# Gate and up products of the two-stream feed-forward blocks by seven half-size products per pair, in a two-layer hybrid diffusion backbone

## The chip, the cores and the metric

One Trainium2 core runs the whole network in one launch. The metric is the device time of that launch in microseconds (us), smaller being better. Engines are named as in the profile: PE is the matrix engine (TensorE), PEld its weight loads, DVE the vector engine, ACT the scalar engine, POOL is GpSimd, and SP issues the DMAs.

## The reference

Two token streams of 256 tokens each (contexts `cx`, latents `x`), 1024 channels and two layers with the same weights for both streams; everything is float32. Cut to what matters here:

```python
for layer in range(DEPTH):                       # 2
    mx = jnp.split((silu_c @ ada_w[layer] + ada_b[layer])[:, None, :], N_MOD, axis=-1)   # 9 modulations, latents
    mc = ...                                     # the same from silu_cc, contexts
    x  = x  + 0.5 * mx[2] * swiglu(modulate(rmsnorm(x,  norm_w[layer, 0]), mx[0], mx[1]), ffn1_wgu[layer], ffn1_wd[layer])
    cx = cx + 0.5 * mc[2] * swiglu(modulate(rmsnorm(cx, norm_w[layer, 0]), mc[0], mc[1]), ffn1_wgu[layer], ffn1_wd[layer])
    ...                                          # mixer: retention and gated DeltaNet, gates, output projection
    x  = x  + 0.5 * mx[8] * swiglu(...)          # second FFN; the contexts only where the layer is not the last
return rmsnorm(x, final_norm_w)

def swiglu(h, w_gu, w_down):                     # w_gu: 1024 x 5632, w_down: 2816 x 1024
    gate, up = jnp.split(h @ w_gu, 2, axis=-1)
    return (jax.nn.silu(gate) * up) @ w_down
```

Three of the four feed-forward blocks work on both streams: first and second of layer 0, first of layer 1. They are called FFN(0,0), FFN(0,2) and FFN(1,0) here. FFN(1,2) works on the latents alone.

## The kernel before, in words

Activations lie feature-major: a tile is 128 channels by 512 columns, the contexts in columns 0 to 255 and the latents in 256 to 511. A float32 product is made from three fast ones. Every operand is split into a rounded part hi and the rest lo, and hi times hi, hi times lo and lo times hi are added in PSUM; so each weight tile of 128 by 128 costs three matmuls (`dense`).

Weights come as a stream in the order of use. A DMA brings a unit of 1024 columns (tile `raw`, or two arena tiles `s`), that is two quanta of 512 columns, four weight tiles each. `_ensure` splits quanta ahead of PE: ACT copies the quantum to `wh` (rounded), and DVE subtracts it (`wl <- raw, wh`, L343). Splits run four quanta (`AHEAD`) ahead of the products. For one phase of the mixers every second `wl` is made on POOL (`plo`).

The hidden layer of 2816 has 22 column blocks in two halves of 11. For each half, 11 pairs of a gate block and its up block are made (two blocks of 8 channel tiles, 24 matmuls each, four quanta a pair), then `silu(gate) * up` is split, then the 8 down products of that half (22 quanta) are added to the residual `x` (`x_add`). During the last two down blocks of a feed-forward block (`tail`) and the first products of the next phase (`head`) the two streams run one after the other, so that the next norm is made meanwhile.

The modulations (one row of 1024 channels per layer, index and stream) are made beside the products: `ada_spread` is a generator that `run` interleaves with the products. For each of 8 channel tiles, two halves and two streams it issues one DVE instruction on 512 columns (`s <- s,sc,s`: accumulate a weight tile times a scalar per partition), and yields `GAP` us (1.5 to 2.0) of products. 32 such items, then a few small matmuls, make one modulation. 15 modulations are listed by phase in `SPREAD`.

Instructions reach each engine's queue in the order in which the Python code issues them, and an engine takes its queue in order.

The helpers hold the profile's lines: L274 every matmul, L262 every ACT instruction, L265 and L268 DVE's two-input and scalar-two-input instructions, L343 the `wl` of weights, L723 the sums of squares on POOL.

## Time and profile before

| | us |
|---|---|
| median of 3 runs (2434.14 to 2443.7) | 2438.14 |
| span of the profiled execution | 2433.8 |
| median less that span | 4.3 |

The page gives each engine's busy time over the whole span: PE 98%, PEld 84%, DVE 63%, ACT 41%, POOL 10%. A busy share is an average over phases that differ: feed-forward blocks with 512 columns to a matmul, mixers with many small products, and a last feed-forward block with 256 columns. The windows and the timeline separate them. A matmul's own duration in the profile overlaps with the next one's, so its rate is read from how many there are in a stretch, or from the distance of two instructions that wait for it.

### The profile page before, as it was taken

What the parts mean: (1) busy time and instruction counts of PE and PEld (TensorE: products, weight loads), DVE (VectorE), ACT (ScalarE), POOL (GpSimd) and SP (SyncE); (2) the same over time, 40 slices, a digit from 0 to 9 for tenths busy, and PEclk for the clock granted to TensorE, in tenths of its full rate; (3) what the DMA queues carried; (4) which work ended last, traced back from release to release, by engine and by line L of the source; (5) the groups of instructions that cost most, each with busy time, mean ns of one, the idle gap of its engine ahead of it and who ended that gap; (6) DMA issues with size and microseconds to landing.
All of it is one profiled execution on the core that took longest, in us unless ns stands there. A gap on an engine that the chain in (4) does not pass through costs nothing.

```text
span 2433.8 us, 38580 instructions
## 1 busy us (share of the span) xinstructions
PE 2389.8 (98%) x14930; PEld 2037.7 (84%) x14930; DVE 1529.1 (63%) x2905; ACT 1002.2 (41%) x1998; POOL 241.5 (10%) x256
## 2 busy tenths in 40 slices
PE   7999999999999999999999999999999899999998
PEld 5888888888778888888887897888897789999998
DVE  5776777536775655576656666556465648777654
ACT  4322224344645444342223342223254446555544
POOL 0000001012430200100000100000013322200001
PEclk9999999999999999999999999999999999999999
DMA  8545444322332414444444344444233424546653
GB/s 288 182 172 180 170 156 136 96 87 83 99 97 64 120 44 172 140 141 145 147 159 145 125 144 153 158 139 139 95 112 111 118 96 139 153 138 226 196 177 122
DMA packets 173848, 338.56 MB, mean 139 GB/s; under 512 B 49312, under 2 KB 54240, under 8 KB 173664
## 3 DMA queue, kind: packets, MB, share of 16 engines
q1 hardware_dynamic: 171264, 331.86, 41.2%
q10 hardware_dynamic: 2400, 4.23, 0.6%
q8 instruction: 117, 1.92, 0.3%
q14 instruction: 67, 0.55, 0.1%
HBM read 325.77 MB, written 10.26 MB: 138 GB/s over the span
## 4 chain that ended last, share of the span: by engine, by line
PE 91%; DVE 4%; issue 2%; DMA 2%; ACT 1%; POOL 0%; SPq 0%; DVEq 0%; ACTq 0%; POOLq 0%
PE mm L274 80%; PE mx L274 10%; DVE s L265 1%; DVE s L268 1%; PE mx L278 1%; ACT s L262 1%; DMA raw<-in_w_dram 1%; DVE wl L343 1%; DMA s<-gd 0%; POOL s L1349 0%; ACT wh L262 0%; DVE s L1368 0%; DMA s<-in_x_dram 0%; DVE sub L265 0%; DVE s L723 0%
## 5 line engine op out<-in xcount | busy, mean ns | idle before, releaser
L274 PE MATMUL mm<-s,wh 128*128 128x512 f32 (+1 forms) x6674 | 1785.3, 356 | 3.3 <-ACT s L262 1.6
L274 PEld LDWEIGHTS mm<-s,wh 128*128 128x128 f32 x6674 | 1169.1, 189 | 195.2 <-issue 9.1
L274 PE MATMUL mm<-s,wl 128*128 128x512 f32 (+1 forms) x3337 | 1180.7, 354 | 1.4 <-DVE wl L343 1.3
L274 PEld LDWEIGHTS mm<-s,wl 128*128 128x128 f32 x3337 | 629.5, 189 | 95.5 <-DVE wl L343 2.1
L262 ACT ACTIVATE s<-s 128x512 fp32r<-128x512 f32 (+4 forms) x555 | 274.9, 503 | 612.1 <-DVE s L265 405.4
L343 DVE TENSOR_TENSOR wl<-raw,wh 128x512 fp32r<-128x512 f32 x563 | 399.8, 719 | 101.6 <-ACT wh L262 66.6
L262 ACT ACTIVATE wh<-raw 128x512 fp32r<-128x512 f32 x622 | 374.3, 625 | 207.1 <-PE mm L274 144.0
L268 DVE SCALAR_TENSOR_TENSOR s<-s,sc,s 128x512 f32<-128x512 f32 x420 | 303.4, 748 | 0.0
L262 ACT ACTIVATE s<-mm 128x512 f32<-128x512 f32 (+2 forms) x177 | 91.3, 516 | 353.0 <-PE mm L274 352.3
L265 DVE TENSOR_TENSOR s<-s,s 128x512 fp32r<-128x512 f32 (+3 forms) x300 | 169.1, 575 | 44.7 <-ACT s L262 41.1
L274 PE MATMUL mx<-s,s 32*32 32x32 f32 (+3 forms) x2680 | 183.2, 243 | 11.0 <-DVE s L265 6.2
L274 PEld LDWEIGHTS mx<-s,s 32*32 32x32 f32 (+2 forms) x2680 | 168.9, 142 | 26.6 <-issue 13.4
L265 DVE TENSOR_TENSOR s<-s,mm 128x512 f32<-128x512 f32 (+1 forms) x88 | 54.6, 621 | 210.7 <-PE mm L274 207.5
L343 DVE TENSOR_TENSOR wl<-s,wh 128x512 fp32r<-128x512 f32 x233 | 164.3, 710 | 25.5 <-ACT wh L262 15.3
L723 POOL TENSOR_TENSOR s<-s,s 128x512 f32<-128x512 f32 (+1 forms) x31 | 38.0, 1226 | 1379.1 <-ACT s L262 1037.8
L262 ACT ACTIVATE wh<-s 128x512 fp32r<-128x512 f32 x234 | 140.4, 622 | 75.1 <-PE mm L274 67.8
L268 DVE SCALAR_TENSOR_TENSOR s<-mm,mods,s 128x256 f32<-128x256 f32 x132 | 58.9, 479 | 123.5 <-PE mm L274 123.4
L343 POOL TENSOR_TENSOR wl<-raw,wh 128x512 fp32r<-128x512 f32 x59 | 78.5, 1333 | 219.9 <-ACT wh L262 196.7
L268 DVE SCALAR_TENSOR_TENSOR s<-mm,par,s 128x508 f32<-128x508 f32 (+3 forms) x128 | 90.7, 711 | 13.7 <-ACT s L262 11.1
L262 ACT ACTIVATE s<-mx 128x256 f32<-128x256 f32 (+5 forms) x122 | 53.5, 447 | 76.2 <-PE mx L274 59.4
L274 PE MATMUL mm<-wh,s 128*128 128x512 f32 x256 | 81.2, 398 | 1.3 <-DVE s L977 1.1
L274 PE MATMUL mm<-s,s 128*128 128x256 f32 (+1 forms) x624 | 82.1, 291 | 0.0
(158 smaller groups left out, 1108.5 us busy)
## 6 DMA issues: line engine op xcount, KB each, us to landing
raw<-in_w_dram SPq DMA_DIRECT2D x318, 512.0 KB, 3.6
s<-in_ada_dram SPq DMA_DIRECT2D x288, 256.0 KB, 4.9
s<-in_w_dram SPq DMA_DIRECT2D x244, 256.0 KB, 5.3
s<-in_tab_dram SPq DMA_DIRECT2D x18, 256.0 KB, 4.0
xd<-s SPq DMA_DIRECT2D x16, 256.0 KB, 3.8
s<-gd ACTq DMA_DIRECT2D x16, 256.0 KB, 5.0
s<-in_x_dram SPq DMA_DIRECT2D x8, 256.0 KB, 5.4
yd<-s SPq DMA_DIRECT2D x8, 256.0 KB, 3.7
```

The costliest lines, as they stand in the source:

```text
L262: return self.nc.scalar.activation(out, in_, f, **kw)
L265: return self.nc.vector.tensor_tensor(out, a, b, op)
L268: return self.nc.vector.scalar_tensor_tensor(out, a, s, b, op0=op0, op1=op1)
L274: return self.nc.tensor.matmul(out, lhsT, rhs, start=start, stop=stop, **kw)
L278: return self.nc.tensor.transpose(out, in_, self.ident[:n, :n])
L343: eng.tensor_tensor(lo, self.raw[s // 2][0][s % 2], hi.bitcast(F32), ALU.subtract)
L723: eng.tensor_tensor(acc[:, n0:n1], acc[:, n0:n1], s[:, n0:n1], ALU.add)
```

## The change

Lines of the changed kernel are those of its own file: matmuls are L341, ACT L329, DVE's L332 and L335, the weights' `wl` L457.

For 49 of the 66 pairs of the three two-stream blocks, gate and up of a column block are made as a 2 by 2 block product (rows: gate, up; inner: even and odd channel tiles; columns: contexts, latents) by seven half-size products instead of eight, Strassen's scheme in Winograd's form. `FAST` gives the number of pairs that stay as they were: 11 and 0 in the halves of FFN(0,0), 3 and 0 in FFN(0,2) and in FFN(1,0). Each of the seven (`pairs`) has four channel tiles, three matmuls each, and 256 columns. Its weights are one of a11, a12, a22 (as they come) or one of four sums s1 to s4 that POOL makes from the raw weights (`_sum`, issued `LEAD` quanta ahead of the split). So a pair has seven quanta to split instead of four. Its activations are the tiles of one stream, or sums over streams and even and odd tiles that `xforms` makes once for each feed-forward block: 16 POOL instructions of 256 columns and 8 splits. Two PSUM tiles per pair, `a` and `b`, collect the products; `a` is copied out by ACT in between, while it goes on collecting.

The modulations become one list for the whole kernel. `background` advances it by time after each step of the products of a feed-forward block, at `gap` 1.6 or 1.8 us per item in plain pairs, 6.0 in the new pairs and 1.1 in the down products; in the down products every second item goes to ACT and POOL (`bgpool`). Up to 7 modulations are made in FFN(0,0) and in the first part of the first mixer (gap 3.0), the others in FFN(0,2) and FFN(1,0).

```diff
-SPREAD = {(0, 0): [(0, 2), (0, 3), (0, 4), (0, 5), (0, 6), (0, 7)], (0, 2): [(0, 8), (1, 0), (1, 1), (1, 2), (1, 3)],
-          (1, 0): [(1, 4), (1, 5), (1, 6), (1, 7)], (1, 2): []}
-GAP = {(0, 0): 1.5, (0, 2): 1.8, (1, 0): 2.0, (1, 2): 2.0}
+FAST = {(0, 0): (11, 0), (0, 2): (3, 0), (1, 0): (3, 0)}
+FORMS = ("a11", "a12", "s2", "s1", "s3", "s4", "a22")
+LEAD = 3
+SPREAD = [(0, i) for i in range(2, 9)] + [(1, i) for i in range(8)]
+RATE = (1.8, 6.0, 1.1), True
+RATES = {(0, 0, 0): ((1.6, 6.0, 1.1), True)}
+MIX_RATE = 3.0
+FIRST_MODS = 7
...
+    def _sum(self, s):
...
+        while self.presum and self.presum[0][0] <= s + LEAD:
+            _, u, f = self.presum.popleft()
+            d = self.sums[u]
+            (a11, a12), (a21, a22) = self.raw[u][0], self.raw[u + 1][0]
+            a, b, op = {"s1": (a21, a22, ALU.add), "s2": (d.get("s1"), a11, ALU.subtract),
+                        "s3": (a11, a21, ALU.subtract), "s4": (a12, d.get("s2"), ALU.subtract)}[f]
+            d[f] = self.A()
+            self.nc.gpsimd.tensor_tensor(d[f], a, b, op)
...
-            self.act(hi, src)
+            self._sum(s)
+            self.act(hi, self._src(s))
...
-            eng.tensor_tensor(lo, self.raw[s // 2][0][s % 2], hi.bitcast(F32), ALU.subtract)
+            eng.tensor_tensor(lo, self._src(s), hi.bitcast(F32), ALU.subtract)
...
+                        if st and self.bgpool:
+                            t = self.A() if k else a
+                            self.act(t, raw, AF.Copy, scale=c)
+                            if k:
+                                self.nc.gpsimd.tensor_tensor(a, a, t, ALU.add)
+                                self.Fr(t)
+                        elif k:
+                            self.stt(a, raw, c, a)
...
+    def xforms(self):
...
+        sub = lambda o, a, b: self.nc.gpsimd.tensor_tensor(o, a, b, ALU.subtract)
+        for i in range(5):
...
+                sub(p[:, lc], e[:, rc], e[:, lc])
+                sub(p[:, rc], o[:, rc], p[:, lc])
+                sub(r[:, lc], o[:, rc], e[:, rc])
+                sub(r[:, rc], o[:, lc], p[:, rc])
+                self.Fr(e, o)
+            if pend:
+                self.X.append([self.split(t, 0, 512, 0, 1) for t in pend])
...
+    def pairs(self, n, hid):
...
+            a, b = self.mm()[:, lc], self.mm()
+            g, c = self.A(), self.A()
...
+            prod(a, even, lc, True, False)
+            self.act(g[:, lc], a)
+            yield 1.42
+            prod(b[:, lc], odd, lc, True, False)
+            yield 1.42
+            prod(a, x1, rc, False, False)
+            self.act(g[:, rc], a)
+            yield 1.42
+            prod(b[:, rc], x1, lc, False, False)
+            self.act(c[:, rc], b[:, rc])
+            yield 1.42
+            prod(a, x2, lc, False, False)
+            self.act(c[:, lc], a)
+            self.nc.gpsimd.tensor_tensor(c[:, lc], c[:, lc], c[:, rc], ALU.add)
+            yield 1.42
+            prod(b[:, rc], odd, rc, False, True)
+            self.tt(g, g, b, ALU.add)
+            post.append(lambda: self.act(g, g, AF.Silu))
+            yield 1.42
+            prod(a, x2, rc, False, True)
+            self.nc.gpsimd.tensor_tensor(g[:, rc], g[:, rc], c[:, lc], ALU.mult)
+            self.tt(g[:, lc], g[:, lc], a, ALU.mult)
+            self.Fr(c)
+            hid.append(self.split(g, 0, 512, 0.5, 1))
+            yield 1.42
...
-            yield from self.dense([1] * 22 if half else G_FFN if l + j else G_START, KD, self.hk, n0, n1, ev)
+            rate, pool = RATES.get((l, j, half), RATE)
+            fast = (l, j) in FAST
+            self.gap, self.bgpool = rate[0], False
+            if fast and half == 0:
+                self.xgen = self.xforms()
+            for w in self.dense(_plain_groups(l, j, half), KD, self.hk, n0, n1, ev):
+                if fast and self.xgen:
+                    self.xgen = next(self.xgen, 0) is None and self.xgen
+                yield w
...
+                self.gap = rate[1]
+                yield from self.pairs(HH - _plain(l, j, half), hid)
+            self.gap, self.bgpool = rate[2], pool
```

What PE has in its queue in the second half of FFN(0,2), before (`s` are the split activations, `mm` the PSUM tile of one block, `wh` and `wl` one quantum of weights):

```order
L274 MATMUL mm_12326<-s10_9746,wh_12210 128x512
L274 MATMUL mm_12326<-s70_9747,wh_12210 128x512
L274 MATMUL mm_12326<-s10_9746,wl_12239 128x512
L274 MATMUL mm_12326<-s30_9766,wh_12210 128x512
L274 MATMUL mm_12326<-s8_9767,wh_12210 128x512
L274 MATMUL mm_12326<-s30_9766,wl_12239 128x512
```

The same place after the change, from a pair's fourth product to its fifth, where `mm_13977` and `mm_13976` are the collecting tiles `b` and `a` of one pair:

```order
L341 MATMUL mm_13977<-s29_11103,wh_13933 128x256
L341 MATMUL mm_13977<-s51_11104,wh_13933 128x256
L341 MATMUL mm_13977<-s29_11103,wl_13957 128x256
L341 MATMUL mm_13976<-s22_10956,wh_13953 128x256
L341 MATMUL mm_13976<-s75_10957,wh_13953 128x256
L341 MATMUL mm_13976<-s22_10956,wl_13984 128x256
```

Each matmul has half the columns, and 84 of them stand where 48 stood; each quantum of `wh` and `wl` still serves 12 matmuls.

DVE's queue at the same place before, about one pair long (`sc` marks an item of a modulation, `s49_12228,mm_12236` is silu(gate) times up):

```order
L343 TENSOR_TENSOR wl_12239<-s23_12018,wh_12210 128x512
L268 SCALAR_TENSOR_TENSOR s21_12179<-s26_12175,sc_164,s21_12179 128x512
L343 TENSOR_TENSOR wl_12256<-s25_12019,wh_12237 128x512
L265 TENSOR_TENSOR s49_12228<-s49_12228,mm_12236 128x512
L268 SCALAR_TENSOR_TENSOR s71_12181<-s26_12175,sc_164,s71_12181 128x512
L343 TENSOR_TENSOR wl_12282<-s34_12059,wh_12254 128x512
L265 TENSOR_TENSOR s61_12276<-s49_12228,s48_12275 128x512
L268 SCALAR_TENSOR_TENSOR s1_12180<-s63_12176,sc_164,s1_12180 128x512
L268 SCALAR_TENSOR_TENSOR s54_12182<-s63_12176,sc_164,s54_12182 128x512
L343 TENSOR_TENSOR wl_12305<-s57_12060,wh_12280 128x512
```

And after, one pair of the second half of FFN(0,2) (`s45_13978,mm_13977` adds PSUM tile `b`, `s45_13978,mm_13976` multiplies by `a`, `s58_14119` is the lo of the hidden tile):

```order
L457 TENSOR_TENSOR wl_14062<-raw_13734,wh_14042 128x512
L457 TENSOR_TENSOR wl_14082<-s30_13981,wh_14060 128x512
L332 TENSOR_TENSOR s45_13978<-s45_13978,mm_13977 128x512
L457 TENSOR_TENSOR wl_14101<-s42_13954,wh_14080 128x512
L332 TENSOR_TENSOR s45_13978<-s45_13978,mm_13976 128x256
L457 TENSOR_TENSOR wl_14128<-s37_14001,wh_14097 128x512
L335 SCALAR_TENSOR_TENSOR s68_13619<-s53_13950,sc_164,s68_13619 128x512
L457 TENSOR_TENSOR wl_14151<-s15_14020,wh_14124 128x512
L332 TENSOR_TENSOR s58_14119<-s45_13978,s36_14118 128x512
L457 TENSOR_TENSOR wl_14170<-raw_13770,wh_14147 128x512
L457 TENSOR_TENSOR wl_14189<-raw_13879,wh_14166 128x512
L457 TENSOR_TENSOR wl_14206<-raw_13879,wh_14187 128x512
```

Seven `wl` stand between two hidden tiles instead of four, one or two modulation items instead of six or so, and a second instruction that reads PSUM.

POOL has nothing in its queue before in the pairs; after, in the second half of FFN(0,2) (L405 are the sums s1 to s4 of the next pair's weights, L1078 the sum of two halves of `c`, L1085 the product with silu(gate) for the latents):

```order
L1078 TENSOR_TENSOR s21_12952<-s21_12952 128x256
L405 TENSOR_TENSOR s7_13070<-s43_12865,s58_12866 128x512
L1085 TENSOR_TENSOR s15_12951<-s15_12951,s21_12952 128x256
L405 TENSOR_TENSOR s34_13097<-s7_13070,s67_12814 128x512
L405 TENSOR_TENSOR s53_13117<-s67_12814,s43_12865 128x512
L405 TENSOR_TENSOR s42_13136<-s9_12815,s34_13097 128x512
L1078 TENSOR_TENSOR s74_13095<-s74_13095 128x256
```

Each pair has come to have four POOL instructions of 512 columns and two of 256.

## Rows read from the trace of the kernel before

**Rows 1.** The page: span, and busy time (share) and instructions of each engine.

```profile
span 2433.8 us, 38580 instructions
PE 2389.8 (98%) x14930; PEld 2037.7 (84%) x14930; DVE 1529.1 (63%) x2905; ACT 1002.2 (41%) x1998; POOL 241.5 (10%) x256
```

**Rows 2.** The page: the chain that ended last, shares by engine.

```profile
PE 91%; DVE 4%; issue 2%; DMA 2%; ACT 1%; POOL 0%; SPq 0%; DVEq 0%; ACTq 0%; POOLq 0%
```

**Rows 3.** Windows: down FFN(0,2), pairs FFN(0,2), pairs FFN(1,0), FFN(1,2), first mixer's start.

```profile
core 0: us, PE busy (x) PEld busy (x) DVE busy (x) ACT busy (x) POOL busy (x), PEclk, DMA share, GB/s
1166.00:1221.00 55.00, 55.00 (x252) 44.15 (x252) 33.33 (x61) 12.58 (x20) 0.00 (x0) 1.00 0.50 170
1232.00:1346.00 114.00, 114.00 (x517) 91.07 (x516) 70.67 (x122) 33.17 (x60) 0.00 (x0) 1.00 0.45 156
1610.00:1724.00 114.00, 114.00 (x518) 91.14 (x517) 67.33 (x113) 33.06 (x60) 0.00 (x0) 1.00 0.39 130
2250.00:2390.00 140.00, 140.00 (x1190) 140.00 (x1189) 83.59 (x152) 69.56 (x139) 0.00 (x0) 1.00 0.57 185
410.00:620.00 210.00, 210.00 (x1091) 175.83 (x1089) 110.82 (x194) 95.37 (x199) 27.78 (x25) 1.00 0.26 83
```

**Rows 4.** Timeline of DVE, a pair of FFN(0,2): start, length, idle before and its releaser.

```profile
1277.78 0.69 DVE L265 TENSOR_TENSOR s<-s,mm 128x512 f32<-128x512 f32 x1 [3.46 <-PE mm L274]
1278.38 0.75 DVE L268 SCALAR_TENSOR_TENSOR s<-s,sc,s 128x512 f32<-128x512 f32 x1
1279.04 0.68 DVE L343 TENSOR_TENSOR wl<-raw,wh 128x512 fp32r<-128x512 f32 x1
1279.64 0.68 DVE L265 TENSOR_TENSOR s<-s,s 128x512 fp32r<-128x512 f32 x1
...
1288.91 0.69 DVE L265 TENSOR_TENSOR s<-s,mm 128x512 f32<-128x512 f32 x1 [3.46 <-PE mm L274]
```

**Rows 5.** Timeline of DVE, a pair of FFN(1,2) (latents alone, 256 columns).

```profile
2353.03 0.42 DVE L265 TENSOR_TENSOR s<-s,mm 128x256 f32<-128x256 f32 x1 [1.20 <-PE mm L274]
2353.37 0.68 DVE L343 TENSOR_TENSOR wl<-s,wh 128x512 fp32r<-128x512 f32 x1
...
2358.69 0.42 DVE L265 TENSOR_TENSOR s<-s,mm 128x256 f32<-128x256 f32 x1 [1.20 <-PE mm L274]
```

**Rows 6.** Timeline of POOL and DVE, end of the first mixer.

```profile
1008.31 4.70 POOL L723 TENSOR_TENSOR s<-s,s 128x512 f32<-128x512 f32 x3 [79.14 <-ACT s L262]
1009.05 1.10 DVE L343 TENSOR_TENSOR wl<-s,wh 128x512 fp32r<-128x512 f32 x1
1010.35 1.50 DVE L343 TENSOR_TENSOR wl<-s,wh 128x512 fp32r<-128x512 f32 x1 [0.20 <-ACT wh L262]
```

**Rows 7.** Timeline of POOL and DVE in the second mixer.

```profile
1836.00 1.30 POOL L343 TENSOR_TENSOR wl<-raw,wh 128x512 fp32r<-128x512 f32 x1 [1.32 <-ACT wh L262]
1835.15 2.42 DVE L268 SCALAR_TENSOR_TENSOR s<-mm,par,s 128x510 f32<-128x510 f32 x4
```

**Rows 8.** Groups by line and shape, whole span: count, busy us, mean ns, idle before.

```profile
L723 POOL TENSOR_TENSOR s<-s,s 128x256 f32<-128x256 f32 x12 | 9.5, 796 | 229.5 <-ACT s L262 229.3
L262 ACT ACTIVATE wh<-raw 128x512 fp32r<-128x512 f32 x622 | 374.3, 625 | 207.1 <-PE mm L274 144.0 <-DMA raw<-in_w_dram 47.4 <-DVE wl L343 7.5
L262 ACT ACTIVATE s<-mm 128x256 f32<-128x256 f32 x66 | 25.0, 379 | 39.0 <-PE mm L274 38.9
```

**Rows 9.** The page: DMA issues of the weights, KB each, us to landing.

```profile
raw<-in_w_dram SPq DMA_DIRECT2D x318, 512.0 KB, 3.6
```

More of the change, by code (lines that the diff above doesn't have):

```diff
@@ L227, in __init__ @@
         self.nunits = ins["w"].shape[0]
+        self.plan = _plan(self.nunits)
+        self.nplan = len(self.plan)
+        self.nfreed, self.npre = 0, 0
+        self.sums, self.presum = {}, deque()
+        self.keepv, self.vs, self.xgen = False, {}, None
+        self.ready = set()
+        self.gap, self.bgt = None, 0.0
+        self.bgpool, self.bgmax = False, FIRST_MODS
+        self.bg = self.ada_spread()
         self.raw, self.hl = {}, {}
@@ L478, in head, with background @@
         self.steps = None
+    def background(self, dt):
+        if self.gap is None or self.bg is None:
+            return
+        self.bgt -= dt
+        while self.bgt <= 0 and self.bg:
+            w = next(self.bg, None)
+            if w is None:
+                self.bg = None
+            else:
+                self.bgt += w
     def run(self, dense, *mixers, scale=1.0):
@@ new lines, in ada_spread, with load @@
+    def ada_spread(self):
+        nxt, todo = [], deque((n, l, i, half, k) for n, (l, i) in enumerate(SPREAD) for half in range(2) for k in range(8))
+        def load():
+            if todo and todo[0][0] < self.bgmax:
+                _, l, i, half, k = todo.popleft()
+                nxt.append(self.A())
+                self.nc.sync.dma_start(nxt[-1], self.ins["ada"][l, i, k, half])
+        for l, i in SPREAD:
+            while not nxt:
+                load()
+                load()
+                yield 2.0 if nxt else 0.7
+            s = self.A()
+            for half in range(2):
+                acc = self.As(2)
+                for k in range(8):
+                    raw = nxt.pop(0)
+                    for st in range(2):
+                        a, c = acc[st], self.sc[:, k, st:st + 1]
+                        if st and self.bgpool:
[6 more added lines that the diff above has]
+                            self.stt(a, raw, c, a)
+                        else:
+                            self.nc.vector.tensor_scalar_mul(a, raw, c)
+                        yield self.gap
+                    self.Fr(raw)
+                    load()
+                yield 1.0
+                ps = self.mx()
+                for st in range(2):
+                    for j in range(2):
+                        p = 64 * half + 32 * j
+                        self.mat(ps[p:p + 32, 0:256], self.sel[:, st], acc[st][:, j * 256:j * 256 + 256], st == 0, st == 1)
+                self.Fr(*acc)
+                self.nc.vector.tensor_copy(s[64 * half:64 * half + 64, :256], ps[64 * half:64 * half + 64, :256])
+            self.ada_rows(l, i, s)
+            yield self.gap
```

191 lines of the change are left out of this document (139 added, 52 removed).

## The prediction

> **What bounds the kernel now.** I read the page first. PE is busy 98% of a span of 2433.8 us [rows 1], and the chain that ended last runs through PE for 91% [rows 2]; DVE has 63% and POOL 10%, so over the whole span PE is the bound and nothing else is near. The windows say the same of the stretches that change: in the pairs of FFN(0,2) and FFN(1,0) PE is busy for all 114 us, DVE for 70.67 and 67.33 of them, ACT for 33, POOL for none [rows 3]. The timeline gives the rate. DVE's multiplication by the up block waits for PE, and one pair later does so again: from 1277.78 to 1288.91, 11.13 us for 48 matmuls of 512 columns [rows 4]. FFN(1,2) has the same pairs with 256 columns: from 2353.03 to 2358.69, 5.66 us for 48 matmuls [rows 5], and PE is busy for all 140 us of its window, with as many weight loads [rows 3]. So half the columns cost half the time (0.118 us a matmul against 0.232), and DVE and ACT keep up with a quantum every 1.41 us.
>
> **A pair by PE alone.** 84 matmuls at 0.118 us are 9.91 us instead of 11.13: 1.22 us a pair, 59.8 us for 49 pairs. Nothing can give more, since the small matmuls of the modulations only move. The Trainium skill (TensorE: Matmul & The Clock Gate, Part 3, The mechanism) says that a weight load overlaps running matmuls only where the row groups differ. Here all are 128 by 128, so by it loads and matmuls would add: by the same page (Part 2, LDWEIGHTS) 128 columns at 1.2 GHz, an estimated 0.107 us more for each of 84, and the sum would be 9 us a pair longer than mine. The window of FFN(1,2) does not agree: 1190 matmuls and 1189 loads within 140 us leave no time between them [rows 3]. I take the row.
>
> **A pair by DVE and POOL together.** This term decides. At the end of the first mixer three POOL additions stand in one row of 4.70 us, and the two `wl` of DVE beside them take 1.10 and 1.50 us [rows 6] instead of 0.68 [rows 4]. In the second mixer a POOL instruction of the same size takes 1.30 us beside DVE instructions that read PSUM, which take 2.42 us for four, as fast as alone [rows 7]. So a DVE instruction with both inputs in SBUF and a POOL instruction don't run at once. What each holds the other up for: 4.70 less 1.30 is 3.40 for two rounds of one `wl` and one addition, 1.70 a round. A `wl` behind another DVE instruction comes 0.60 us before the next (1279.04 to 1279.64), a modulation item 0.66 (1278.38 to 1279.04) [rows 4]. That leaves 1.10 for a POOL instruction of 512 columns. One of 256 takes 0.80 [rows 8], 0.50 less than 1.30, so 0.60.
>
> In a new pair DVE has seven `wl` and the lo of the hidden tile, 8 x 0.60 = 4.80; modulation items, 7 steps of 1.42 us at one per 6.0, 1.6 x 0.66 = 1.06; POOL has four sums, 4.40, and two halves, 1.20. Together 11.46 us, more than PE's 9.91 and more than the 11.13 of before. Besides, DVE reads PSUM twice, 0.60 [rows 4] and 0.34 [rows 5]; POOL may work meanwhile if it has something ready. So a pair that goes on and on costs 11.46 to 12.40. I take 11.6, near the lower end, since POOL has work for half of the time and both PSUM readings come where one of its sums is queued.
>
> The Trainium skill (SBUF — State Buffer, Who interferes with whom) has the same two instructions exclude each other, for the whole instruction. With whole lengths, 0.68, 0.75, 1.30 and 0.80, a pair would be 13.4 us. The rows above have them closer, 1.70 a round instead of 1.98; that is the measured one, and the page's is a rival below.
>
> **What a stretch of pairs costs.** The stretch is shorter than its number times 11.6. The first pair's four sums (4.40) and four splits (2.4) are done ahead, in a stretch with room. At the end PE needs only its last `wl`; behind it stand four splits for the down products (2.4), two POOL halves (1.2) and a lo (0.6). Together 11.0 us. Eleven pairs: 11 x 11.6 - 11.0 = 116.6 against 122.4 before, -5.8, three times: -17.4. Eight pairs: 92.8 - 11.0 = 81.8 (PE's own floor is 79.3) against 89.0, -7.2, twice: -14.4.
>
> **Ahead of the eight pairs** stand three plain pairs, 12 quanta of 2.78 us, 33.4 us. There the exclusive work is 12 `wl`, 3 hidden lo and 8 lo of the new activation sums (13.8), 16 items (10.6), 16 lo of the norm's halves at 0.34 (5.4), on POOL 16 halves and 4 sums (14.0): 43.8 us, 10.4 too much. Some of it eats the lead of four quanta, and some delays PE: 0 to 10.4, I take 5, twice: +10. In FFN(0,0) the same work has 11 plain pairs to lie in, 122 us, and costs nothing.
>
> **Down products.** 22 quanta are 61 us; PE is busy for all 55 us of the window and DVE for 33 [rows 3]. After the change: 22 `wl` (13.2), some 22 items on DVE (14.5), some 19 on POOL (20.9), six squares in second halves (6.6): 49 to 55 us. This fits and costs nothing; where it doesn't, PE waits for the excess, 6 us at most per half.
>
> **First mixer.** Some 62 items move there, 41 us of DVE into 210 us of which DVE works 110.8 [rows 3]: 0 to 6, I take 2. **ACT** has, per pair, seven splits at 0.63, four copies of halves at 0.38 [rows 8] and two instructions of 512 columns, 7.2 us: it fits. **DMA**: the same bytes, landing in 3.6 us [rows 9]; a unit is asked for some nine quanta before POOL's sum needs it, so nothing; without that lead a sum would come late, and the split behind it on ACT.
>
> **Sum.** -17.4 - 14.4 + 10 + 2 = -19.8: 2433.8 becomes 2414. The median lies 4.3 us above the profiled span, so 2418.
>
> **Rivals.**
> *PE sets the pace* (0.18): DVE and POOL overlap better than three rows show, or POOL's work slips between. All 59.8 us come, less 2 in the mixer: 2380. For it: FFN(1,2) runs at that pace without POOL [rows 5]; against it: [rows 6].
> *POOL and DVE don't fill each other's gaps* (0.25), the one that ends slower: a pair is 12.4, eleven pairs are 125.4 (+3.0, three times), eight 88.2 (-0.8, twice), the plain stretches +10.4 twice, the mixer +6: +34, 2472. It decides from about 12.0 us a pair, for 49 x 0.4 is all of my gain. For it: POOL's `c` sum and product wait for ACT, and DVE for silu, in queues taken in order.
> *ACT's copy of a collecting tile comes late* (0.08): the third product writes `a` again, and product two covers 1.41 us; the copy takes 0.38 behind a split of 0.63 [rows 8]. If that split waits for a sum on POOL, PE stops: 0.5 us a pair is 25 us, 2443, three such a pair 2492.
> *Whole lengths exclude each other* (0.05): 13.4 us a pair, 1.8 x 49 = 90 more than my sum, 2506.
>
> **How the numbers follow.** My case has 0.44 and its own range 2398 to 2440. Differences below 0.5% (12 us) can't be told from none. Faster by more: the first rival and seven tenths of my case, 0.50. Within: the rest of my case, and the near ends of the second and third rival, 0.20. Slower: 0.30. The range of 8 in 10 reaches to the first and to the second rival, 2382 to 2474.
>
> **What would show it.** In the profile after: matmuls of 256 columns in the pairs with idle PE time before them, ended by DVE's `wl`, and a pair's period near 11.6; POOL rows near 6 us of each pair; `wl` lengthened from 0.68 to 1.1 and more on average; DVE near 9 tenths there. If the period is 9.9 and PE never idle, the exclusive term is wrong; if it is over 12, the overlap with PSUM readings is. If PE waits for ACT's copies rather than for `wl`, the third rival holds. Idle PE before the first new pairs of FFN(0,2) and FFN(1,0) would show the plain stretches' excess. A longer first mixer, by more than 6 us, would make the prediction wrong in a place where I gave it little.

## The result and the profile after

The changed kernel takes 2553.49 us (median of 4 runs, 2552.28 to 2555.24) beside 2437.81 us of the kernel before: a ratio of 1.0474 [1.0458, 1.0490], 116 us slower. The forecast was 2418, and its range ended at 2474.

The page of the changed kernel, its span and busy times, answers to [rows 1]:

```profile
span 2553.5 us, 43820 instructions
PE 2403.4 (94%) x16694; PEld 2118.9 (83%) x16694; DVE 1891.5 (74%) x3016; ACT 1237.6 (48%) x2489; POOL 866.9 (34%) x707
```

PE's busy time has hardly changed (2389.8 before), though the new pairs should take some 60 us off it, while DVE has 362 us more and POOL 625. The windows of the changed kernel answer to [rows 3]. They are the second down products of FFN(0,0), the first of FFN(0,2), the head and plain pairs of FFN(1,0), and some ten new pairs each of FFN(0,2) and of FFN(1,0):

```profile
core 0: us, PE busy (x) PEld busy (x) DVE busy (x) ACT busy (x) POOL busy (x), PEclk, DMA share, GB/s
359.60:434.30 74.70, 61.83 (x301) 50.66 (x301) 46.14 (x65) 28.62 (x49) 36.15 (x25) 0.89 0.45 156
1226.60:1288.60 62.00, 59.59 (x266) 46.33 (x265) 47.60 (x64) 24.26 (x39) 35.72 (x23) 0.97 0.48 166
1299.00:1417.00 118.00, 104.68 (x840) 102.06 (x839) 114.11 (x120) 63.89 (x132) 75.37 (x55) 0.97 0.34 113
1488.00:1533.00 45.00, 32.90 (x206) 28.37 (x205) 38.18 (x56) 23.64 (x49) 31.81 (x28) 0.85 0.15 48
1714.00:1832.00 118.00, 106.05 (x866) 103.61 (x865) 114.66 (x121) 64.28 (x133) 77.06 (x57) 0.99 0.34 114
```

In the pairs DVE is now the full engine (97%), as foreseen. But PE idles in all five windows, down products and heads included, and its granted clock is below 1.00 in each of them. Where the time went shows best by phases. A phase is bounded here by the first and the last of DVE's residual additions (`s<-mm,mods,s`, or `x_add` in the code) of each down product and of the first mixer's output product (24 us, in the head of FFN(0,2)). A head ends with the first `silu(gate)*up`. The columns hold times from the profiled execution of each kernel, in us. The last five are experiments that follow; in the last one the stretches of the fourth row hold five new pairs each, not eight.

| phase | before | after | list alone | no sums | sums on DVE | list mended | six plain |
|---|---|---|---|---|---|---|---|
| start to first down product | 160.4 | 168.6 | 164.8 | 166.5 | 168.0 | 165.8 | 166.2 |
| gate/up with 11 new pairs, three | 397.1 | 403.7 | 397.6 | 353.7 | 356.7 | 359.6 | 361.2 |
| gate/up with 8 new pairs, two | 220.9 | 224.6 | 225.9 | 202.4 | 205.0 | 203.5 | 214.3 |
| down products, six halves | 324.3 | 377.8 | 358.4 | 367.8 | 374.6 | 337.5 | 331.2 |
| heads of FFN(0,2), FFN(1,0) | 75.7 | 110.4 | 80.4 | 102.3 | 102.5 | 102.2 | 78.8 |
| first mixer | 603.9 | 613.0 | 611.6 | 612.4 | 611.8 | 616.8 | 612.4 |
| second mixer, FFN(1,2) | 641.5 | 644.3 | 637.1 | 646.3 | 644.0 | 643.6 | 644.7 |

The pairs lose 10 us where I had a gain of 31.8. The down products lose 53.5 where I had nothing, and the heads 34.7 where I had 10. The start loses 8.2 where I had nothing.

**The pairs.** DVE's timeline in FFN(0,2), from one addition of tile `b` to the next, answers to [rows 4]:

```profile
1359.06 0.68 DVE L332 TENSOR_TENSOR s<-s,mm 128x512 f32<-128x512 f32 x1
...
1363.50 1.77 DVE L332 TENSOR_TENSOR s<-s,s 128x512 fp32r<-128x512 f32 x1
1365.19 1.78 DVE L335 SCALAR_TENSOR_TENSOR s<-s,sc,s 128x512 f32<-128x512 f32 x1
...
1370.95 0.67 DVE L332 TENSOR_TENSOR s<-s,mm 128x512 f32<-128x512 f32 x1
```

POOL in the same stretch:

```profile
1360.60 0.73 POOL L1085 TENSOR_TENSOR s<-s,s 128x256 f32<-128x256 f32 x1 [2.02 <-ACT s L329]
1361.29 5.14 POOL L405 TENSOR_TENSOR s<-s,s 128x512 f32<-128x512 f32 x3
1367.35 0.83 POOL L1078 TENSOR_TENSOR s<-s 128x256 f32<-128x256 f32 x1 [0.92 <-ACT s L329]
```

The pair takes 11.89 us; the mean of eight, from 1299.20 to 1395.62, is 12.05. Beside three POOL sums DVE's instructions last 1.77 us instead of 0.68, one every 1.70. Then POOL stands idle for 0.92 us and more, since its additions of halves wait for ACT. It was idle too, for 2.02 us up to 1360.60, while DVE read PSUM at 1359.06. In the eight pairs DVE reads PSUM for 8.73 us, and POOL works beside only 4.29 of them.

ACT and PE in the same stretch:

```profile
1359.83 0.63 ACT L329 ACTIVATE s<-s 128x512 f32<-128x512 f32 x1 [3.12 <-DVE s L332]
...
1361.37 0.63 ACT L329 ACTIVATE s<-s 128x512 fp32r<-128x512 f32 x1 [0.38 <-POOL s L1085]
1361.90 0.36 ACT L329 ACTIVATE s<-mm 128x256 f32<-128x256 f32 x1
```

```profile
1362.32 0.51 PE L341 MATMUL mm<-s,wh 128*128 128x256 f32 x2 [1.40 <-ACT s L329]
```

ACT waits 3.12 us for DVE's addition of tile `b`, makes silu and, after POOL's product, the hidden tile's hi; only then comes the copy of the collecting tile that PE has been waiting for. So the full DVE reaches PE by way of ACT. Over the eight pairs ACT waits for DVE's additions 22.5 us (8 times), and no split of ACT waits for a sum on POOL.

**PE's waits**, over the whole span (engine, tile, line, and what ended the wait; us in total, times, longest):

```profile
PE mm L341 <- ACT s L329: 54.2, 37, 2.4
PE mm L341 <- DVE s L332: 24.5, 10, 5.8
PE mx L341 <- DVE s L335: 13.8, 8, 3.4
PE mx L341 <- POOL s L754: 12.7, 8, 3.5
```

The first row is the pairs: PE waits for ACT's copies of the collecting tile. The second is mostly the norm at the heads (19 us of it). The last two are the matmuls that select a modulation's rows, which wait for its last item, made by DVE (L335) or POOL (L754). PE's timeline in the second down products of FFN(0,0):

```profile
375.47 0.63 PE L341 MATMUL mx<-s,sel 128*32 128x256 f32 x4 [3.49 <-POOL s L754]
...
376.83 1.00 PE L341 MATMUL mm<-s,wh 128*128 128x512 f32 x2
...
381.16 0.63 PE L341 MATMUL mm<-s,wh 128*128 128x512 f32 x2
```

The four small matmuls stand in PE's queue ahead of all that follows, so PE stops for 3.49 us. Behind the stop, two matmuls of 512 columns take 1.00 us instead of 0.63, because the granted clock has fallen to its lower level, 1.2 GHz. A window of this stretch shows it:

```profile
376.80:380.30 3.50, 3.50 (x10) 2.70 (x9) 1.49 (x3) 0.00 (x0) 0.00 (x0) 0.51 0.00 0
```

Why the item is late stands in DVE's and POOL's timelines before it:

```profile
366.02 0.75 DVE L335 SCALAR_TENSOR_TENSOR s<-s,sc,s 128x512 f32<-128x512 f32 x1 [3.59 <-DMA s<-in_ada_dram]
```

```profile
371.20 1.65 POOL L865 TENSOR_TENSOR s<-s,s 128x512 f32<-128x512 f32 x1 [2.68 <-ACT s L329]
372.81 2.60 POOL L754 TENSOR_TENSOR s<-s,s 128x512 f32<-128x512 f32 x2
```

DVE waited 3.59 us for the modulation's weights, whose next load is issued only when an earlier half is used up. POOL's additions of items stood behind the sum of squares of the next norm (L865), which itself waited for ACT.

### The profile page after: what moved, and what is told of

Same layout as the page of the kernel before. It is cut to its first block, busy times and chain, and to the rows that moved or that the text cites. A ratio compares the mean times of both kernels' runs of the same rounds, so it can differ in the third digit from the quotient of the medians.

```text
span 2553.5 us, 43820 instructions
## 1 busy us (share of the span) xinstructions
PE 2403.4 (94%) x16694; PEld 2118.9 (83%) x16694; DVE 1891.5 (74%) x3016; ACT 1237.6 (48%) x2489; POOL 866.9 (34%) x707
## 5 line engine op out<-in xcount | busy, mean ns | idle before, releaser
L341 PE MATMUL mm<-s,wh 128*128 128x256 f32 (+1 forms) x7850 | 1810.8, 326 | 62.3 <-ACT s L329 54.2
L341 PEld LDWEIGHTS mm<-s,wh 128*128 128x128 f32 x7850 | 1311.1, 191 | 202.2 <-ACT s L329 63.7
L341 PE MATMUL mm<-s,wl 128*128 128x256 f32 (+1 forms) x3925 | 1269.3, 323 | 3.4 <-issue 2.6
L341 PEld LDWEIGHTS mm<-s,wl 128*128 128x128 f32 x3925 | 750.7, 191 | 64.4 <-issue 2.9
L329 ACT ACTIVATE s<-s 128x512 fp32r<-128x512 f32 (+4 forms) x628 | 318.8, 518 | 545.0 <-DVE s L332 323.1
L457 DVE TENSOR_TENSOR wl<-raw,wh 128x512 fp32r<-128x512 f32 x534 | 427.0, 814 | 94.8 <-ACT wh L329 76.4
L329 ACT ACTIVATE wh<-raw 128x512 fp32r<-128x512 f32 x593 | 358.7, 625 | 143.5 <-PE mm L341 84.8
L457 DVE TENSOR_TENSOR wl<-s,wh 128x512 fp32r<-128x512 f32 x409 | 396.1, 983 | 25.7 <-ACT wh L329 16.3
L335 DVE SCALAR_TENSOR_TENSOR s<-s,sc,s 128x512 f32<-128x512 f32 x311 | 308.0, 998 | 56.8 <-DMA s<-in_ada_dram 56.5
L329 ACT ACTIVATE s<-mm 128x256 f32<-128x256 f32 (+2 forms) x324 | 136.2, 420 | 300.6 <-PE mm L341 293.4
L332 DVE TENSOR_TENSOR s<-s,s 128x512 fp32r<-128x512 f32 (+3 forms) x324 | 243.0, 766 | 34.7 <-ACT s L329 31.7
L329 ACT ACTIVATE wh<-s 128x512 fp32r<-128x512 f32 x410 | 245.7, 621 | 20.2 <-PE mm L341 18.4
L754 POOL TENSOR_TENSOR s<-s,s 128x512 f32<-128x512 f32 x109 | 170.1, 1560 | 236.3 <-ACT s L329 126.1
L341 PE MATMUL mx<-s,s 32*32 32x32 f32 (+3 forms) x2680 | 181.9, 241 | 8.6 <-DVE s L332 7.0
L341 PEld LDWEIGHTS mx<-s,s 32*32 32x32 f32 (+2 forms) x2680 | 167.7, 140 | 24.6 <-issue 10.3
L457 POOL TENSOR_TENSOR wl<-raw,wh 128x512 fp32r<-128x512 f32 x59 | 78.3, 1327 | 240.1 <-PE mm L341 153.5
L865 POOL TENSOR_TENSOR s<-s,s 128x512 f32<-128x512 f32 (+1 forms) x31 | 37.1, 1197 | 360.3 <-ACT s L329 356.4
L329 ACT ACTIVATE s<-s,sc 128x512 f32<-128x512 f32 x124 | 87.7, 715 | 116.1 <-DMA s<-in_ada_dram 98.9
L332 DVE TENSOR_TENSOR s<-s,mm 128x256 f32<-128x256 f32 (+1 forms) x137 | 74.4, 543 | 54.9 <-PE mm L341 48.2
L405 POOL TENSOR_TENSOR s<-s,s 128x512 f32<-128x512 f32 x67 | 112.2, 1684 | 3.9 <-DVE wl L457 2.7
L335 DVE SCALAR_TENSOR_TENSOR s<-mm,mods,s 128x256 f32<-128x256 f32 x132 | 58.6, 476 | 64.0 <-PE mm L341 63.7
L341 PE MATMUL mm<-s,s 128*128 128x256 f32 (+1 forms) x624 | 87.3, 298 | 12.3 <-DVE s L332 12.2
```

The costliest lines, as they stand in the source:

```text
L329: return self.nc.scalar.activation(out, in_, f, **kw)
L332: return self.nc.vector.tensor_tensor(out, a, b, op)
L335: return self.nc.vector.scalar_tensor_tensor(out, a, s, b, op0=op0, op1=op1)
L341: return self.nc.tensor.matmul(out, lhsT, rhs, start=start, stop=stop, **kw)
L405: self.nc.gpsimd.tensor_tensor(d[f], a, b, op)
L457: eng.tensor_tensor(lo, self._src(s), hi.bitcast(F32), ALU.subtract)
```

## The experiments

All times are medians, each beside runs of the kernel before on the same chip; a ratio is to that kernel.

**The list without the pairs.**

```diff
-FAST = {(0, 0): (11, 0), (0, 2): (3, 0), (1, 0): (3, 0)}
+FAST = {}
```

> Nothing is left out: all 66 pairs run as in the kernel before (two weight quanta by both streams), and only the one modulation list, half of its items on POOL, is kept from the change. Theory A (the list stops PE: its selecting matmuls stand in PE's queue and wait for late items, in the down products above all): 2475 to 2495 us, the halves of down products stay near 62 to 75 us instead of 55. Theory B (the list is innocent; the new pairs' sums and splits are the loss): 2435 to 2445 us, down products back at 55 us.

Measured: 2492.66 us, 1.0214 [1.0196, 1.0231]. So the list alone costs 52 us, and the pairs another 61 on top. That is the first theory; the second had at most 2445. The first halves of down products are less hurt than I wrote (55.3, 60.9 and 53.8 us). The loss is in the second halves of FFN(0,0) (66.3) and FFN(0,2) (70.6). There PE waits for the norm's squares on POOL as well, in whose queue the list's additions now stand. PE's timeline there:

```profile
1421.30 0.63 PE L341 MATMUL mx<-s,sel 128*32 128x256 f32 x4 [1.14 <-POOL s L754]
...
1448.10 1.01 PE L341 MATMUL mx<-ones,s 128*128 128x1 f32 x4 [4.72 <-POOL s L854]
1452.81 1.01 PE L341 MATMUL mx<-ones,s 128*128 128x1 f32 x4 [3.69 <-ACT s L329]
```

**No POOL sums.** The four instructions of `_sum` are dropped; s1 to s4 are split from the raw tile instead.

> Left out: POOL's four weight sums of each new pair (196 instructions); the seven quanta are split from unsummed tiles, so the products are other ones. Theory of the port (DVE and POOL exclude each other, 4.4 us of POOL a pair): the pairs fall from about 12.0 us to 9.9 to 10.5, the stretches of eleven to 112 to 118, and the whole to 2455 to 2485 us. Rival (PE waits for ACT's copy of the collecting tile whatever POOL does): pairs stay at 11.5 us or more, 2530 to 2555 us.

Measured: 2461.06 us, 1.0082 [1.0063, 1.0101]. The pairs run at PE's own pace. A window of some ten pairs of FFN(0,2):

```profile
1254.00:1356.00 102.00, 102.00 (x865) 101.25 (x864) 75.47 (x119) 64.38 (x133) 15.57 (x21) 1.00 0.39 132
```

PE never idles, and a pair takes 9.9 us, or 11.1 where the selection of a modulation falls into it. PE's waits for ACT's copies fall from 54.2 us to 2.2, though ACT does the same work. So ACT's copies were not the cause; they stood in ACT's queue behind silu, which waited for the full DVE. DVE is now busy for 75.47 of 102 us, and ACT's waits for its additions are 8.4 us in this window, none longer than 0.8.

**Seven of eight list steps left out.**

```diff
-for half in range(2) for k in range(8))
+for half in range(2) for k in range(1))
...
-                for k in range(8):
+                for k in range(1):
```

> Left out: seven of eight steps of each modulation of the list (their loads and their items); the selecting matmuls, their copies and all else stay. Theory A (late items hold PE's queue): the down products return to 55 or 56 us a half (-50), the mixers to their time of before (-10), the pairs gain the items' share of the port, 0.7 us each (-30): 2455 to 2480 us. Theory B (only the pairs lose): -30 alone, 2515 to 2530 us.

Measured: 2458.57 us, 1.0079 [1.0062, 1.0096]. The down products return to 323.5 us in all (324.3 before; one half, the first of FFN(0,2), still takes 61.7) and the first mixer to 604.5, as the first theory has it. Pairs in the middle of a stretch still take 11.3 us, so items explain only 0.7 us of a pair. The start became 12 us longer than after the change. I did not settle why; the list runs eight times as fast there, and its selections stand closer together.

**All items on DVE.**

```diff
-RATE = (1.8, 6.0, 1.1), True
-RATES = {(0, 0, 0): ((1.6, 6.0, 1.1), True)}
+RATE = (1.8, 6.0, 1.1), False
+RATES = {(0, 0, 0): ((1.6, 6.0, 1.1), False)}
```

> All items of the modulation list are made by DVE, none by ACT and POOL; the rest is the changed kernel. Theory A: POOL's additions come late behind squares and lengthen DVE's items beside them; without them the down products return to 56 to 60 us a half, 2505 to 2525 us in all. Theory B: the items' engine does not matter, 2545 to 2560 us. A third case: DVE itself is overfull with all items, 2560 us and more.

Measured: 2527.21 us, 1.0361 [1.0342, 1.0381], 26 us less than after the change; the down products take 355.7 us. The time lies just above the first case, and well below the second.

**Selection later.** In `ada_spread` the selecting matmuls and their copy become a function `sel` that is deferred:

```diff
+                def sel(l=l, i=i, half=half, acc=acc, s=s):
...
+                self.defer(3, sel)
```

> The selecting matmuls of each modulation of the list and their copy are issued three quanta later than in the changed kernel, when the last items should be done; nothing is left out. Theory A (PE's queue stops at them because the items are late): PE's waits there go from 35 us to under 8, and the time to 2505 to 2530 us. Rival (the items' loads come late and hold ACT and DVE, so the next weight splits are late whatever PE does): 2540 to 2555 us.

Measured: 2533.48 us, 1.0393 [1.0374, 1.0412]. PE no longer waits at a selection, but only 20 us come back, and the down products still take 356.9. DVE's and ACT's waits for the modulations' weights are as long as before (55.4 and 94.5 us). The time lies just above the first case. What is left in these down products is not PE waiting for weight splits: there it waits for the squares of the next norm on ACT and POOL (up to 3.6 us at a time), its granted clock is 0.94 and 0.95 in two of the halves, and the selecting matmuls themselves take longer than before (below).

**Loads further ahead.**

```diff
                 load()
                 load()
+                load()
+                load()
                 yield 2.0 if nxt else 0.7
```

> The modulation list keeps four half loads ahead instead of two; nothing is left out. If late loads of the modulation weights are what makes the items late in the down products: ACT's and DVE's waits for these loads (99 and 57 us) mostly vanish, the down products fall by 25 to 45 us in all, 2510 to 2530 us. If the lateness is POOL's queue and the port: 2540 to 2555 us.

Measured: 2524.83 us, 1.0354 [1.0334, 1.0375]. ACT's wait for these loads falls from 98.9 us to 3.3 and DVE's from 56.5 to none; 29 us come back. POOL's items still stop PE, 7.5 us in all. So each of the three changes to the list takes away a part of the loss, and none takes away all of it.

**Sums asked for earlier.**

```diff
-LEAD = 3
+LEAD = 5
```

> POOL's weight sums are asked for five quanta ahead instead of three; nothing is left out. Theory of the port (POOL and DVE have more work than a pair lasts): the period stays at 11.8 to 12.2 us, 2545 to 2560 us. Rival (a sum is only late: it stands on POOL behind the c sum that waits for ACT, ACT's split waits for it, and the copy of the collecting tile behind that): the period falls below 11.3 us, 2500 to 2525 us.

Measured: 2537.19 us, 1.0407 [1.0387, 1.0428]; the mean of eight pairs is 11.34 us (1289.47 to 1380.23). It lies between the two: 0.7 us of the 2.1 that a pair has above 9.9 comes back. But this was not a late sum that PE waited for. In these eight pairs PE idles for 10.07 us, beside 10.43 after the change. What falls is DVE's busy time, from 94.34 us to 86.53, and POOL now works beside 7.99 of the 8.08 us in which DVE reads PSUM, where it was 4.29 of 8.73. PE is busy for 80.63 us instead of 85.97, at a granted clock of 0.98 instead of 0.96.

**Sums on DVE.**

```diff
-            self.nc.gpsimd.tensor_tensor(d[f], a, b, op)
+            self.nc.vector.tensor_tensor(d[f], a, b, op)
```

> The four weight sums of a new pair are made by DVE instead of POOL; the rest is the changed kernel, nothing is left out. Theory of the port (a POOL instruction of 512 columns costs DVE about 1.1 us of its time, the same sum on DVE about 0.60): the pair falls from 12.0 us to 10.0 to 10.5 and the whole to 2465 to 2500 us. Rival (DVE has no room for 2.4 us more a pair: its queue is the bound in the pairs whoever adds): pairs stay at 12 us or get longer, 2550 us and more.

Measured: 2477.05 us, 1.0162 [1.0145, 1.0179], 76 us less than after the change, for moving 196 instructions to the engine that was full. DVE's timeline in FFN(0,2):

```profile
1308.16 0.69 DVE L405 TENSOR_TENSOR s<-raw 128x512 f32<-128x512 f32 x1
1308.76 0.69 DVE L457 TENSOR_TENSOR wl<-s,wh 128x512 fp32r<-128x512 f32 x1
```

A sum takes DVE 0.60 us from its start to the next instruction's; on POOL it took DVE away for longer. The mean of eight pairs is 10.16 us (1266.56 to 1347.83).

**Idle POOL sums.** To tell contention from lateness, POOL makes sums that nobody needs beside the sums on DVE.

```diff
             self.nc.vector.tensor_tensor(d[f], a, b, op)
+            if self.scr is None:
+                self.scr = self.A()
+            self.nc.gpsimd.tensor_tensor(self.scr, self.con[:, :512], self.con[:, 128:640], ALU.add)
```

> The kernel with the sums on DVE (2477 us), and POOL makes beside each of them a sum of the same size from constants into a tile that nobody reads: 196 POOL instructions that no weight, split or product waits for. Nothing is left out. Theory of the port (POOL's instruction itself holds DVE up, whoever needs its result): wl beside them go from 0.7 to 1.1 us and more, pairs from 9.9 to 11 to 13 us, 2520 to 2580 us in all. Rival (what costs is only that a sum comes late on POOL): pairs stay at 9.9 to 10.5 us, 2470 to 2485 us.

Measured: 2656.82 us, 1.0885 [1.0869, 1.0900]: 180 us more than the kernel with the sums on DVE, 0.92 us for each of the 196. DVE's timeline in FFN(0,0):

```profile
303.63 1.78 DVE L405 TENSOR_TENSOR s<-s,raw 128x512 f32<-128x512 f32 x1
305.33 1.77 DVE L460 TENSOR_TENSOR wl<-s,wh 128x512 fp32r<-128x512 f32 x1
307.02 0.68 DVE L332 TENSOR_TENSOR s<-s,s 128x512 fp32r<-128x512 f32 x1
```

And POOL's:

```profile
301.43 5.12 POOL L408 TENSOR_TENSOR s<-con 128x512 f32<-128x512 f32 x3
307.47 0.83 POOL L1081 TENSOR_TENSOR s<-s 128x256 f32<-128x256 f32 x1 [0.92 <-ACT s L329]
```

While POOL's three run (301.43 to 306.55), DVE's instructions come every 1.70 us; once they have ended, one lasts 0.68 again. Nothing waits for these sums, so they cost by their mere running. The mean of eight pairs is 14.23 us (1344.58 to 1458.38), 4.07 more than without them, 1.02 for each of four. That is more than either case had. POOL's halves stand behind the idle sums in its queue, so lateness could still be a rival; but DVE is never idle in these pairs, as their window shows, so its own lengthened instructions are the bound:

```profile
1344.00:1458.00 114.00, 87.69 (x682) 82.58 (x682) 114.00 (x127) 50.63 (x104) 68.30 (x49) 0.99 0.27 87
```

The five stretches of pairs hold 155 of the 180 us. PE now waits for `wl` itself:

```profile
PE mm L341 <- DVE wl L460: 66.7, 49, 2.3
```

**Sums of activations on DVE alone.** In `xforms`, `gpsimd` becomes `vector`; the rest is the changed kernel.

> The changed kernel with only the sixteen sums of activations of an FFN made by DVE instead of POOL. Nothing is left out. If they are what makes the heads of FFN(0,2) and FFN(1,0) 15 and 19 us longer: 2518 to 2535 us. Rival (the weight sums of the first pairs and the items do it): 2545 to 2556 us.

Measured: 2548.10 us, 1.0454 [1.0429, 1.0479]. The heads fall by 4 us of 35, so these sums' place on POOL is not what makes the heads long.

**The list mended**: sums on DVE, items on DVE, three loads ahead, selection deferred.

> Sums on DVE, and the list mended in three ways at once: all its items on DVE, three half loads kept ahead instead of two, the selecting matmuls three quanta later. Nothing is left out. Alone, the first gave 2477, and the others 26, 29 and 20 us less than the changed kernel. If these three cure different stops, they add: 2400 to 2415 us. If they cure the same lateness of the items: 2430 to 2450 us, with the down products at 56 to 60 us a half. Third case (DVE is overfull with sums and items): 2465 us and more, pairs above 10.5 us.

Measured: 2441.10 us, 1.0007 [0.9998, 1.0017]. The three together gave 36 us, not the 75 of the single ones (with four loads ahead in the run alone). That fits the second case, one lateness that each of them cures in part, though the down products were only some 50 us too long, so that not all of 75 could come. The down products take 337.5 us, and the five stretches of pairs together 563.1 instead of 561.7, so DVE is not overfull.

**The same, with the sums of activations on DVE**, and then **with the items spread otherwise**:

```diff
-RATE = (1.8, 6.0, 1.1), False
-RATES = {(0, 0, 0): ((1.6, 6.0, 1.1), False)}
-FIRST_MODS = 7
+RATE = (1.8, 4.0, 1.4), False
+RATES = {(0, 0, 0): ((1.5, 4.0, 1.4), False), (0, 0, 1): ((1.8, 4.0, 1.7), False), (0, 2, 1): ((1.8, 4.0, 1.7), False), (1, 0, 1): ((1.8, 4.0, 1.7), False)}
+FIRST_MODS = 6
```

> The kernel of the mended list, with the sixteen sums of activations of an FFN made by DVE as well. Nothing is left out. If POOL's rows of 3.3 us there hold DVE's norm back at the head of FFN(0,2) and FFN(1,0): 15 to 25 us less than the mended list without it. If the heads are long because of weight sums, items and splits that all stand in DVE's queue: no change, within 6 us.

> The kernel before this one, with the items spread otherwise: one per 1.4 us in first and 1.7 in second down products instead of 1.1, one per 4.0 in the new pairs instead of 6.0, six modulations before the end of the first mixer instead of seven. Nothing is left out. If items crowd DVE in the down products: another 10 to 25 us less, down products at 54 to 57 us, 2385 to 2410 us in all. If the pairs have no room for one more item each: pairs go to 10.5 us, and nothing is won.

Measured: 2434.46 us, 0.9982 [0.9969, 0.9994], and 2432.17 us, 0.9969 [0.9957, 0.9981]. Both gains are smaller than expected. The first, 7 us, is near the case of no change; the second, 2 us, is not clear of the noise: the down products fall by 7.4 us, but the pairs take 4.6 more and the second mixer with what follows it 3.3. The heads are still 21 us too long in the second. PE's timeline at the head of FFN(1,0) in that kernel:

```profile
1419.65 1.69 PE L341 MATMUL mm<-s,s 128*128 128x256 f32 x12 [1.37 <-DVE s L332]
1423.65 4.51 PE L341 MATMUL mm<-s,s 128*128 128x256 f32 x23 [2.31 <-DVE s L332]
1431.06 0.80 PE L341 MATMUL mm<-s,wh 128*128 128x512 f32 x1 [2.66 <-DVE s L332]
```

And the window around it:

```profile
1405.00:1437.00 32.00, 25.66 (x167) 23.02 (x167) 31.33 (x75) 19.14 (x39) 1.02 (x1) 0.89 0.15 50
```

DVE is busy for 31.33 of 32 us, and PE waits for the norm's lo.

**Heads cleared.** The sums of activations begin only when all eight channel tiles of the norm are made. Ahead of FFN(1,0) the list also pauses.

```diff
+                done = (l, j) == (0, 0) or (min(self.made) if self.made else len(self.h)) == 8
+                self.gap = rate[0] if done or (l, j) not in [(1, 0)] else None
-                if fast and self.xgen:
+                if fast and self.xgen and done:
```

> The kernel with the spread items (2432 us), with the sums of activations of FFN(0,2) and FFN(1,0) begun only when all channel tiles of the norm are made, and with no items from the last two down products before FFN(1,0) until then. Nothing is left out. If DVE's queue is what makes the heads long (before them 26 us, there 37.6 ahead of FFN(1,0) and 10 too long ahead of FFN(0,2)): the head of FFN(1,0) falls to 28 to 32 us and that of FFN(0,2) by 3 to 6 us, 2415 to 2425 us in all. If it is the norm's own chain or the first pair's sums: no change, 2428 to 2436 us.

Measured: 2438.73 us, 0.9995 [0.9984, 1.0007]. The heads are short again (78.1 us for both, 26.2 for that of FFN(1,0)), so it was DVE's queue. But the stretches behind them take 221.5 us instead of 205.8, and the second mixer 8 us more for the items that moved there. The work had only moved; my total was wrong.

**More plain pairs.** The same without the pause, with five and with six plain pairs ahead.

```diff
-FAST = {(0, 0): (11, 0), (0, 2): (3, 0), (1, 0): (3, 0)}
+FAST = {(0, 0): (11, 0), (0, 2): (6, 0), (1, 0): (6, 0)}
```

> The kernel with the spread items, its sums of activations begun only after the norm's tiles, and five plain pairs instead of three ahead of the new ones in FFN(0,2) and FFN(1,0): 45 new pairs in all. Nothing is left out. The sums of activations, their splits and the first four weight sums are some 13 us of DVE; a plain pair leaves DVE about 4 us free, so three pairs behind the norm's two give them room. If that is why the heads are long: heads near 26 us and the pairs behind at 9.9 us, 2410 to 2422 us. If they only move along (as when the sums were begun later with three plain pairs): 2432 us or more.

> The same with six plain pairs there and 43 new ones. If five already give the room, this is 2 to 3 us longer than with five; if not, shorter.

Measured: 2422.35 us, 0.9937 [0.9925, 0.9949], and 2418.26 us, 0.9920 [0.9905, 0.9934]. Six measures 4 us less than five, but their intervals overlap, and the phases do not say that five gave too little room: the heads take 78.5 us with five and 78.9 with six, and the stretches behind 212.1 and 214.3, 2.2 longer with six, as the first case has it. With six new pairs fewer the ratio falls from the 0.9969 of the kernel with spread items to 0.9920: the heads fall by 17.8 us, while the stretches behind grow by 8.6. With three plain pairs and the list paused the heads were as short, but the stretches behind took 221.5 us; so DVE finds room for the preparation in the plain pairs. The later sums without the pause were not run with three plain pairs. The version with six beats the kernel before by 0.8% and the changed one by 5.3% (2418.26 against 2553.49). PE is back at 98% of the span, and the pairs there are near PE's pace, as a window of some ten of them in FFN(0,2) shows:

```profile
1232.00:1337.00 105.00, 104.18 (x873) 102.14 (x872) 100.94 (x168) 64.21 (x133) 24.46 (x21) 1.00 0.42 136
```

DVE is at 96% in it, so little more fits into these pairs.

## Why the prediction was wrong

The forecast was -19.8 us on the span, and the span grew by 119.7. Of the 139.5 us between them the pairs are 42.1, the down products 53.5, the heads 24.7, the start 8.2, the first mixer 7.1, and the second mixer with what follows 3.9.

**PE alone, 9.91 us a pair: right.** Without the sums a pair takes 9.9 us.

**DVE and POOL together, 11.46 to 12.40 us, taken as 11.6: the mechanism right, the value 0.45 low.** It measured 12.05. A POOL instruction of 512 columns costs DVE 1.02 to 1.10 us (four idle ones lengthened a pair by 4.07; 1.70 a round less 0.60), as [rows 6] gave. What I had wrong is how well the two fill each other's gaps: I let both PSUM readings of DVE fall where POOL is at work, and only half of their time did (4.29 of 8.73 us). With the sums asked for earlier nearly all of it does, and a pair takes 11.34, at the lower end of my range. So the second rival's mechanism is part of it, with 12.05 of its 12.4. By my own sign the third rival held as well, since PE waits for ACT's copies and not for `wl`: 54.2 us, 1.1 a pair. But its reason, a split that waits for a sum on POOL, is not in the trace. The copies stand behind silu, and silu waits for DVE.

**"11.0 us" of lead in each stretch: too much.** Eleven pairs at 12.05 would be 132.6 us. FFN(0,2) lost 3.9 us on its 122.4, which makes 126.3, so the lead was some 6 us; in the stretches of FFN(0,0) and FFN(1,0), which lost 1.7 and 1.0, it was 8 to 9. With both errors the five stretches came out at +10 instead of -31.8.

**Down products, "this fits and costs nothing": the step that failed, 53.5 us.** I counted instructions against the window, 49 to 55 us of 61, and let 6 us a half be the most it could cost. The count was not far off (DVE is busy for 47.60 of 62 us). What I left out is order, and PE's own share. Over the six halves PE's idle time grows from 1.4 to 27.5 us and its busy time from 322.75 to 350.24.

The idle time is order. The selecting matmuls and the norm's small matmuls stand in PE's queue and wait there for late items and late squares from the queues of DVE, ACT and POOL. A late load or a late sum of squares therefore stops PE whatever room the engines have. The nine quanta of lead that I wrote are those of weight units; for the loads of the modulations I had no term, and this list keeps only two half loads.

The busy time is the clock behind such stops (below), and the selecting matmuls. I had written that they "only move". But the kernel before selects both halves of a modulation at once, sixteen matmuls in 1.07 us, and the list selects each half by itself, eight in 1.06. Before and after, over the whole span:

```profile
L274 PE MATMUL mx<-s,sel 128*32 128x256 f32 x240 | 16.1, 385 | 0.0
L341 PE MATMUL mx<-s,sel 128*32 128x256 f32 x240 | 35.9, 409 | 26.5 <-DVE s L335 13.8 <-POOL s L754 12.7
```

In the down products they keep PE busy for 19.72 us instead of 5.35. Even with the list mended they take 31.7 us in all, so selecting by halves costs some 16 us in every version that has the list.

With earlier loads, DVE alone and a deferred selection the down products fell to 337.5 us, and with fewer items in them to 331.0.

**Plain pairs and heads, "0 to 10.4, I take 5" each: 15.2 and 19.5.** I set the excess against the twelve quanta of plain pairs. But it falls on the norm, whose tiles PE needs one by one; PE stops at once (9.2 and 9.9 us of waits for DVE in the two heads, with a granted clock of 0.85 in the window of the second), and there is no lead to eat. With sums, items and all on DVE 21 us remained; room for the preparation in three more plain pairs brought it to 3.

**First mixer, +2: measured 9.1.** With one list step in eight it took 604.5, in all other runs 611 to 617, so the cost is the list's. I sized it by DVE's free time there. But PE itself is busy 6.4 us longer (606.50 instead of 600.08), and 5.4 of that are the forty selecting matmuls that moved there. How many items there are does not set it: the list alone has 20 there instead of 65, and took 611.6. Items that moved into the second mixer cost 8 and 16 us there in two runs.

**FFN(0,0)'s plain pairs, "costs nothing": 8.2 in the start.** The list alone makes it 4.4 longer; where the rest comes from is open.

**The clock was in no term** (below).

## What to carry to other kernels

Before moving work to an idle engine, price what it takes from its neighbour: a two-input instruction on POOL cost DVE more time (1.02 to 1.10 us) than doing it on DVE itself (0.60). When work is put between products of a full matrix engine, counting busy time is not enough: follow each of its results to the in-order queue where it is awaited, and ask what loads it and what stands behind it. Count those small matmuls again when their grouping changes. Prepare a faster form of a product where the preparing engine has room, even if fewer products get it; forty-three such pairs were faster than forty-nine (0.9920 of the kernel before against 0.9969).

## What the runs showed of the hardware

POOL's cost does not depend on anyone who waits for it. DVE instructions with both inputs in SBUF come every 0.60 us alone [rows 4], and a POOL instruction of 512 columns lasts 1.30 beside DVE instructions that read PSUM [rows 7]. Together they alternate at 1.70 us a round, even with idle sums of constants on POOL.

The Trainium skill (SBUF — State Buffer, Who interferes with whom) has the two exclude each other for whole instructions. The exclusion agrees; the whole lengths, 1.98 with DVE's 0.68, do not, since a round measured 1.70.

A stop of PE costs more than itself. After the stop of 3.49 us above, the granted clock was 0.51 for 3.5 us. Over the span its mean fell from 0.995 to 0.979. With only a full and a half level (2.4 and 1.2 GHz) that is an estimated 24 us at the lower one before (1.0% of 2433.8) and 107 after (4.2% of 2553.5). At half speed the 83 us between them cost up to 41 us of PE's work, at most about a third of the whole loss. In the second down products of FFN(0,0), at 0.89, PE idles for 12.87 of the 74.70 us and is busy for 61.83, where before it was busy for 52.61 of 54.00; slower work adds to the stops themselves. In the version with six plain pairs the mean is 0.995 again.

The Trainium skill (TensorE: Matmul & The Clock Gate, Part 1) says that the lower rate is the default and that activity releases it. The window at 0.51 behind PE's stop agrees.
